# RWKV's inverse placed elsewhere in the program, SiLU and one gate written with tanh, and the first products of a hybrid layer regrouped

## The chip, the cores and the metric

The kernel runs on one core of a Trainium2 chip. The core has five engines with queues of their own: TensorE for matrix products (PE in the profile; PEld are its weight loads), VectorE (DVE), ScalarE (ACT), GpSimd (POOL) and SyncE (SP), which here issues nearly all transfers. Every engine takes its instructions in the order of its queue. The metric is the device time of one execution in microseconds (us); lower is better.

## The reference, cut to what matters

One layer of a decoder with three token mixers on the same input, x of 256 tokens by 2048 channels. One projection of x gives the columns of all mixers and three merge gates:

```python
proj = einsum('bsd,dc->bsc', x, w_in)
z_a, xbc, dt_raw, u_b, z_b, p_rkvz, p_w, p_a, p_gate = split(proj, offs)
# Mamba-2 (SSD): silu(conv(xbc)) gives xs, B, C; y * silu(z_a), then a group norm
# S5: y * sigmoid(y @ w_glu + b_glu) * silu(z_b)
# RWKV-7: r, k, v, z shifted by a token; tanh(xw) @ w2 and xa @ a2 (LoRA); recurrence over tokens; * silu(z)
gates = sigmoid(p_gate + gate_b)
merged = gates[0] * (y_a @ w_a) + gates[1] * (y_b @ w_b) + gates[2] * (y_c @ w_c)
x = layer_norm(alpha * x + merged @ w_out)
```

Here silu(v) = v * sigmoid(v), and sigmoid(v) = (1 + tanh(v / 2)) / 2.

## The kernel before

**Products in three parts.** Every weight column block of 128 is a tile of 2048 x 128 values. `loadw` (line 356) brings it in two halves of 512 KB (`raw`, issued on SP), ScalarE rounds a half to a high part `hi` (line 366), and VectorE subtracts to get the low part `lo` (line 368). x is split the same way once, in eight slabs (`xhi`, `xlo`, lines 308 and 309). `proj` (line 374) then makes 48 products of 128 x 256 into one PSUM tile: hi by xhi, hi by xlo, lo by xhi for 16 slices. There are four buffers each of raw, hi and lo, so two tiles are under way.

**Start.** `setup` (line 298) fetches the slabs of x and, after the first of them, the weights `wd` of the step sizes (32 columns). 48 products of 32 columns give `ps_dt` (lines 317 to 319). The tile `lora`, fetched after x, follows as an ordinary projection (`rwkv_lora`, line 435), then k0, k1 and so on. `par` and `cst`, two tables of constants, are issued at the very start on ScalarE's queue, and five small operations on VectorE prepare scalings from them.

**RWKV.** The 16 heads are worked in four blocks of two pairs. `PROG` (line 81) is the order in which work is emitted: F is a block's front (its projections k, r, v and `rwkv_prep`, which ends in the products `pa` and the masked matrix `Aa`), T the inverse, C the recurrence by chunks, and z, g2 and u are plain projections. In `rwkv_tinv` (line 608) `Aa` goes through DRAM into a layout in which VectorE solves 32 rows one after the other, 31 multiplications `Pm` (line 622) and 31 reductions into `TT` (line 623); the result goes through DRAM again (`Td`, `TTf`); and block products on TensorE, `py` (lines 640 to 649), join the 32 x 32 blocks. Each `py` stands in TensorE's queue at a fixed place, and what stands behind it waits with it. `rwkv_z` (line 711) ends with a SiLU on ScalarE.

**SSD, S5 and the rest.** `PROG2` (line 85) is the order of what follows: S are the eight groups of SSD (`ssd_group`, line 797: four projections x, a convolution, SiLU at line 807, and every other group a block z with SiLU at line 794), s the tiles of S5, zb its gate (SiLU at line 1165), a, b and c the three output branches (`branch`, line 1193; gate a is a sigmoid at line 1202), U the gated unit, G the gates of branch b. ScalarE can evaluate only functions of the table set that it has loaded; `ACT_TABLE_LOAD` changes the set.

**What sets the order.** The program is written for a scheduler that plays it through and places each engine's instructions: what is emitted under `high_priority` (all of `loadw`, shifts, gates) goes first where it is ready, the rest in the order of emission. So an edit in one place can move instructions in others.

Of the kernel before, what the change touches and what calls it, by code (L numbers as in the profile page):

```python
# [1310 lines left out]
```

## Time and profile before

| | us |
|---|---|
| median of 3 runs | 1325.28 (1324.92 to 1326.07) |
| the profiled execution | 1328.45 |
| its span in the trace | 1326.7 |
| PE busy in it | 1278.9 |
| PEld busy | 1202.2 |
| DVE busy | 977.4 |
| ACT busy | 824.0 |

The span runs from the first instruction to the last. A matmul is pipelined: one of 256 columns is shown as 0.28 us long, but the next starts 0.11 us after it, so TensorE can be shown as busy while it waits a little. The granted clock (PEclk) is a share of 2.4 GHz.

### The profile page before, as it was taken

How to read it: one execution, taken by the hardware profiler on the slowest of the kernel's cores; microseconds unless marked ns; L12 is line 12 of the kernel's file. 1: busy time of each engine (PE TensorE's matmuls, PEld its weight loads, DVE VectorE, ACT ScalarE, POOL GpSimd, SP SyncE). 2: the span in 40 equal slices, each digit the busy share in tenths (PEclk: the TensorE clock that was granted, in tenths of full speed). 3: DMA queues.
4: the chain of work that ended last, by engine and by line, in shares of the span. 5: the costliest groups of instructions: out<-in, count | busy, mean ns of one | idle time of the engine just before them, and what ended most of it. 6: DMA issues, size and time to landing. Idle time of an engine off the chain costs nothing.

```text
span 1326.7 us, 27360 instructions
## 1 busy us (share of the span) xinstructions
PE 1278.9 (96%) x10924; PEld 1202.2 (91%) x10924; DVE 977.4 (74%) x1768; ACT 824.0 (62%) x1421; POOL 11.0 (1%) x63
## 2 busy tenths in 40 slices
PE   7999899999999998899999999999999999999996
PEld 7999899999899888798998989999999999999885
DVE  5779887579868646699998656889786665548655
ACT  5677565676645667887768778586655454445430
POOL 1000000000000000000000000000000000000000
PEclk9999999999989998999999999999999999999998
...
GB/s 301 180 167 170 176 161 167 135 133 161 150 170 148 165 150 132 114 191 157 183 171 166 191 165 168 155 152 196 194 176 170 183 184 208 207 225 247 248 176 64
DMA packets 96960, 230.65 MB, mean 174 GB/s; under 512 B 26720, under 2 KB 41536, under 8 KB 96832
## 3 DMA queue, kind: packets, MB, share of 16 engines
...
q10 hardware_dynamic: 432, 0.68, 0.1%
...
HBM read 224.34 MB, written 3.21 MB: 172 GB/s over the span
## 4 chain that ended last, share of the span: by engine, by line
PE 78%; ACT 8%; DVE 5%; DMA 5%; issue 3%; SPq 1%; DVEq 0%; ACTq 0%; POOL 0%; POOLq 0%
PE ps_g L378 7%; PE ps_g L379 7%; PE ps_g L380 7%; PE br L1157 4%; PE br L1156 4%; PE br L1158 4%; PE ps_x L380 2%; PE ps_x L378 2%; PE ps_x L379 2%; PE po L1258 2%; PE po L1259 2%; PE po L1260 2%; PE zq L789 2%; PE zq L790 2%; PE zq L788 2%
## 5 line engine op out<-in xcount | busy, mean ns | idle before, releaser
L378 PE MATMUL ps_g<-xhi,hi_g 128*128 128x256 f32 x768 | 216.2, 281 | 0.0
L379 PE MATMUL ps_g<-xlo,hi_g 128*128 128x256 f32 x768 | 215.2, 280 | 0.0
L380 PE MATMUL ps_g<-xhi,lo_g 128*128 128x256 f32 x768 | 214.7, 280 | 0.0
L368 DVE TENSOR_TENSOR lo_g<-raw_g,hi_g 128x1024 fp32r<-128x1024 f32 x96 | 117.2, 1221 | 63.7 <-ACT hi_g L366 59.4
L366 ACT ACTIVATE hi_g<-raw_g 128x1024 fp32r<-128x1024 f32 x96 | 101.5, 1058 | 93.0 <-PE ps_g L379 70.1
L379 PEld LDWEIGHTS ps_g<-xlo,hi_g 128*128 128x128 f32 x768 | 145.6, 190 | 1.2 <-issue 0.4
L378 PE MATMUL ps_x<-xhi,hi_x 128*128 128x256 f32 x512 | 146.6, 286 | 0.0
L378 PEld LDWEIGHTS ps_g<-xhi,hi_g 128*128 128x128 f32 x768 | 145.4, 189 | 1.3 <-issue 0.4
L380 PE MATMUL ps_x<-xhi,lo_x 128*128 128x256 f32 x512 | 146.3, 286 | 0.0
L380 PEld LDWEIGHTS ps_g<-xhi,lo_g 128*128 128x128 f32 x768 | 145.2, 189 | 0.9 <-issue 0.4
L379 PE MATMUL ps_x<-xlo,hi_x 128*128 128x256 f32 x512 | 144.6, 282 | 0.0
L368 DVE TENSOR_TENSOR lo_x<-raw_x,hi_x 128x1024 fp32r<-128x1024 f32 x64 | 78.2, 1221 | 50.4 <-ACT hi_x L366 50.1
L366 ACT ACTIVATE hi_b<-raw_b 128x1024 fp32r<-128x1024 f32 x64 | 67.6, 1057 | 58.5 <-PE br L1157 33.1
L378 PEld LDWEIGHTS ps_x<-xhi,hi_x 128*128 128x128 f32 x512 | 97.8, 191 | 1.1 <-issue 0.2
L380 PEld LDWEIGHTS ps_x<-xhi,lo_x 128*128 128x128 f32 x512 | 97.5, 190 | 1.0 <-issue 0.2
L379 PEld LDWEIGHTS ps_x<-xlo,hi_x 128*128 128x128 f32 x512 | 97.4, 190 | 0.5
L368 DVE TENSOR_TENSOR lo_b<-raw_b,hi_b 128x1024 fp32r<-128x1024 f32 x64 | 78.2, 1221 | 24.8 <-ACT hi_b L366 23.0
L366 ACT ACTIVATE hi_x<-raw_x 128x1024 fp32r<-128x1024 f32 x64 | 67.5, 1055 | 37.0 <-PE ps_x L379 16.0
L1157 PE MATMUL br<-yh0l,hi_b 128*128 128x256 f32 x256 | 72.2, 282 | 0.0
L1158 PE MATMUL br<-yh0h,lo_b 128*128 128x256 f32 x256 | 72.0, 281 | 0.0
L1156 PE MATMUL br<-yh0h,hi_b 128*128 128x256 f32 x256 | 71.9, 281 | 0.0
L366 ACT ACTIVATE hi_wo<-raw_wo 128x1024 fp32r<-128x1024 f32 x32 | 33.1, 1057 | 42.1 <-PE po L1260 27.3
...
## 6 DMA issues: line engine op xcount, KB each, us to landing
...
```

What stands on the lines that cost most here:

```text
L366: nc.scalar.activation(hi, raw, AF.Copy)
L368: nc.vector.tensor_tensor(lo, raw, hi.bitcast(F32), ALU.subtract)
L378: nc.tensor.matmul(ps, lhsT=hi.k(k), rhs=g.xhi[:, k, :], start=(k == 0), stop=False)
L379: nc.tensor.matmul(ps, lhsT=hi.k(k), rhs=g.xlo[:, k, :], start=False, stop=False)
L380: nc.tensor.matmul(ps, lhsT=lo.k(k), rhs=g.xhi[:, k, :], start=False, stop=(k == NK - 1))
L788: nc.tensor.matmul(ps[tk], lhsT=g.xhi[:, kk, t], rhs=hi.k512(k), start=f0, stop=False)
L789: nc.tensor.matmul(ps[tk], lhsT=g.xhi[:, kk, t], rhs=lo.k512(k), start=False, stop=False)
L790: nc.tensor.matmul(ps[tk], lhsT=g.xlo[:, kk, t], rhs=hi.k512(k), start=False, stop=l0)
L1156: nc.tensor.matmul(ps, lhsT=hi.k(k0 + k), rhs=h, start=(k == 0), stop=False)
L1157: nc.tensor.matmul(ps, lhsT=hi.k(k0 + k), rhs=l, start=False, stop=False)
L1158: nc.tensor.matmul(ps, lhsT=lo.k(k0 + k), rhs=h, start=False, stop=(k == n - 1))
L1258: nc.tensor.matmul(po, lhsT=m[0][:, t], rhs=hi.k512(k), start=f0, stop=False)
```

## The change

1. *Start.* Four products of a zero tile stand first on TensorE. The step sizes' weights are packed into one stationary tile `whl` (32 high columns, 32 low, 64 zero), so that two products a slice take the place of three, and the lora tile is fetched on ScalarE's queue and multiplied in the same loop, slice by slice, as x comes in. `par` and `cst` move behind the slabs and the first weights on SP; the small scalings from them move from VectorE to POOL. The sum of the two step-size halves is made later (`ssd_dt`).
2. *Block products.* `rwkv_tinv` ends with the transfer of `TTf`; `py` is emitted by new entries Y in `PROG`, for blocks 0 and 2 no earlier than a named product of a projection (`BEHIND`) and, with the C after it, at high priority. Front 2 is split into A2 and B2 around them.
3. *SiLU by tanh.* SiLU of the convolution (32 tiles), z of RWKV (8), z of SSD (8) and zb (8) becomes a tanh on ScalarE and one operation more on VectorE, (t + 1) * v, with v halved beforehand; constants make up for factors of two.
4. *Gate a* is a tanh, with the factor taken in later operations.

```diff
-PROG = ("F0 F1 T0 z2 z3 z0 z6 g2_3 z1 C0 T1 g2_1 F2 C1 g2_0 g2_2 g2_4 z4 g2_5 u6 z7 F3 u3 g2_13 g2_14 g2_7 T2 "
-        "g2_15 z5 g2_6 C2 g2_9 g2_8 T3 u5 C3 g2_11 g2_10 u1 u2 u0 u4 u7 g2_12").split()
+PROG = ("F0 F1 T0 z2 z3 z0 z6 g2_3 z1 T1 g2_1 A2 Y0 C0 Y1 B2 C1 g2_0 g2_2 g2_4 z4 g2_5 u6 z7 F3 u3 g2_13 g2_14 g2_7 T2 "
+        "g2_15 z5 g2_6 g2_9 g2_8 u5 g2_11 Y2 C2 T3 Y3 C3 g2_10 u1 u2 u0 u4 u7 g2_12").split()
+BEHIND = {0: ("v4", 23), 2: ("g2_11", 47)}
 PROG2 = ("dt ch S0 S1 S2 S3 c0 c1 s0 c2 s1 c3 c4 c5 c6 c7 c8 c9 c10 c11 c12 s2 c13 c14 c15 S4 S5 S6 zb4 S7 zb0 "
...
+                b = int(st[1:])
+                with tc.high_priority() if b in BEHIND else ExitStack():
+                    with tc.issue_after(g.mms[BEHIND[b][0]][BEHIND[b][1]].ins) if b in BEHIND else ExitStack():
+                        py = rwkv_ty1(g, bts[b], b)
+                    rwkv_ty2(g, bts[b], b, py)
             elif st[0] == "C":
-                rwkv_chunks(g, bts[int(st[1:])], int(st[1:]))
+                with tc.high_priority() if int(st[1:]) in BEHIND else ExitStack():
+                    rwkv_chunks(g, bts[int(st[1:])], int(st[1:]))
             elif st[0] == "g":
                 gate_c(g, int(st.split("_")[1]))
             elif st[0] == "z":
...
-        ps = g.pp.tile([32, T], F32, name="ps_dt", tag="pj", bufs=3)
-        for k in range(NK):
-            nc.tensor.matmul(ps, lhsT=wd[1][:, k, :], rhs=g.xhi[:, k, :], start=(k == 0), stop=False)
-            nc.tensor.matmul(ps, lhsT=wd[1][:, k, :], rhs=g.xlo[:, k, :], start=False, stop=False)
-            nc.tensor.matmul(ps, lhsT=wd[2][:, k, :], rhs=g.xhi[:, k, :], start=False, stop=(k == NK - 1))
...
-    nc.scalar.dma_start(g.par, I["par"])
-    g.cst = g.fix.tile([128, NCST], F32, name="cst")
-    nc.scalar.dma_start(g.cst, I["cst"])
...
+    with tc.high_priority(), tc.tile_pool(name="xp", bufs=1) as xp:
+        zero = xp.tile([128, T], F32, name="zero")
+        nc.vector.memset(zero, 0.0)
+        pz = g.pp.tile([128, T], F32, name="warm", tag="s", bufs=2)
+        nc.scalar.activation(zero[:, 0:1], zero[:, 1:2], AF.Copy)
+        for _ in range(4):
+            nc.tensor.matmul(pz, lhsT=zero[:, 0:128], rhs=zero, start=True, stop=True)
+        wd = xp.tile([128, 16, 32], F32, name="wd")
+        whl = xp.tile([128, 16, 128], F32R, name="whl")
+        nc.gpsimd.memset(whl[:, :, 64:128].bitcast(F32), 0.0)
+        g.adma = nc.scalar.dma_start(wd, I["wdt"])
+        for b in range(8):
...
+            if b == 0:
+                nc.scalar.activation(whl[:, :, 0:32], wd, AF.Copy)
+                nc.vector.tensor_tensor(whl[:, :, 32:64], wd, whl[:, :, 0:32].bitcast(F32), ALU.subtract)
+            if b == 1:
+                g.wlora = loadw(I["wt"][TIDX["lora"]], "lora", eng=nc.scalar)
+        ps = g.pp.tile([128, T], F32, name="ps_dt", tag="pj", bufs=3)
+        pl = g.plora = g.pp.tile([128, T], F32, name="ps_lora", tag="pj", bufs=3)
+        hi, lo = g.wlora
+        for k in range(NK):
+            nc.tensor.matmul(ps, lhsT=whl[:, k, :], rhs=g.xhi[:, k, :], start=(k == 0), stop=False)
+            nc.tensor.matmul(ps, lhsT=whl[:, k, :], rhs=g.xlo[:, k, :], start=False, stop=(k == NK - 1))
+            nc.tensor.matmul(pl, lhsT=hi.k(k), rhs=g.xhi[:, k, :], start=(k == 0), stop=False)
+            nc.tensor.matmul(pl, lhsT=hi.k(k), rhs=g.xlo[:, k, :], start=False, stop=False)
+            nc.tensor.matmul(pl, lhsT=lo.k(k), rhs=g.xhi[:, k, :], start=False, stop=(k == NK - 1))
+        dtx = xp.tile([64, T], F32, name="dtr")
...
+    with tc.issue_after(g.wdma.ins):
+        nc.sync.dma_start(g.par, I["par"])
+        nc.sync.dma_start(g.cst, I["cst"])
...
+    g.hgb = g.fix.tile([128, 88], F32, name="hgb")[:, 0:32]
+    nc.gpsimd.tensor_scalar(g.hgb[:, 0:16], p("gb", 32, 16), 0.5, None, ALU.mult)
+    nc.gpsimd.tensor_scalar(g.hgb[:, 16:32], p("gb", 0, 16), 0.5, None, ALU.mult)
...
+        m = g.mms[n] = []
...
+            m.append(nc.tensor.matmul(ps, lhsT=hi.k(k), rhs=g.xhi[:, k, :], start=(k == 0), stop=False))
...
+def rwkv_ty1(g, bt, b):
+    nc, idn, pys = g.nc, g.c("ident"), []
     for i in range(2):
         py = g.pr.tile([128, 3, NCH, 32], F32, name=f"py{b}_{i}", tag="r", bufs=2)
+        for c in range(NCH):
+            for h, (lo, hi) in enumerate(HS):
+                nc.tensor.matmul(py[lo, 0, c, :], lhsT=bt.TTf[lo, h, i, c, 0:32], rhs=idn[lo, lo], start=True, stop=True)
+        pys.append(py)
+    return pys
...
-    nc.scalar.activation(Z, Z, AF.Silu)
+    t = g.rp.tile([128, T], F32, name=f"zt{hp}", tag="sq2", bufs=2)
+    nc.scalar.activation(t, Z, AF.Tanh)
+    nc.vector.scalar_tensor_tensor(Z, t, 1.0, Z, ALU.add, ALU.mult)
...
-            nc.scalar.activation(g.zs[:, tk, :], ps[tk], AF.Silu)
+            nc.scalar.activation(g.zs[:, tk, :], ps[tk], AF.Tanh, scale=0.5)
+            nc.vector.scalar_tensor_tensor(g.zs[:, tk, :], g.zs[:, tk, :], 1.0, ps[tk], ALU.add, ALU.mult)
 def ssd_group(g, gr):
...
-        nc.scalar.activation(a, a, AF.Silu)
+        th = g.kp.tile([128, T], F32, name=f"th{n}_{gr}", tag="th", bufs=2)
+        nc.scalar.activation(th, a, AF.Tanh)
+        nc.vector.scalar_tensor_tensor(a, th, 1.0, a, ALU.add, ALU.mult)
         cv.append(a)
     if gr % 2 == 0:
...
-            nc.scalar.activation(sg, pg, AF.Sigmoid, bias=g.p("gb", j))
+            nc.scalar.activation(sg, pg, AF.Tanh, scale=0.5, bias=g.hgb[:, 16 + j:17 + j])
     elif br == 1:
         sg = g.sgb[j]
     if j % per == 0:
...
+        elif br == 0:
+            nc.vector.scalar_tensor_tensor(sg, sg, 1.0, pb, ALU.add, ALU.mult)
+            nc.vector.tensor_tensor(acc, acc, sg, ALU.add)
         else:
             nc.vector.tensor_tensor(sg, pb, sg, ALU.mult)
-            if br == 0:
-                nc.vector.scalar_tensor_tensor(acc, acc, 0.5, sg, ALU.mult, ALU.add)
-            else:
-                nc.vector.tensor_tensor(acc, acc, sg, ALU.add)
+            nc.vector.scalar_tensor_tensor(acc, acc, 0.5, sg, ALU.mult, ALU.add)
```

The scheduled orders differ in many places; three matter to the prediction.

VectorE at the end of the first inverse (TT0, Pm0; lo_r4, lo_v4 are low parts of projections, K4 a shift). Before:

```order
L368 TENSOR_TENSOR lo_r4_0_2504<-raw_r4_0_2500,hi_r4_0_2502 128x1024
L622 TENSOR_TENSOR Pm0_1490<-TT0_1489,AT0_1488 128x8x31
L623 TENSOR_REDUCE TT0_1489<-Pm0_1490 128x8
L622 TENSOR_TENSOR Pm0_1490<-TT0_1489,AT0_1488 128x256
L623 TENSOR_REDUCE TT0_1489<-Pm0_1490 128x8
L368 TENSOR_TENSOR lo_r4_1_2510<-raw_r4_1_2506,hi_r4_1_2508 128x1024
L432 SCALAR_TENSOR_TENSOR K4_2410<-ps_k4_2361,par_166,K4_2410 128x255
L368 TENSOR_TENSOR lo_v4_0_2568<-raw_v4_0_2564,hi_v4_0_2566 128x1024
```

After:

```order
L346 TENSOR_TENSOR lo_r4_0_2241<-raw_r4_0_2237,hi_r4_0_2239 128x1024
L677 TENSOR_REDUCE TT0_1484<-Pm0_1485 128x8
L676 TENSOR_TENSOR Pm0_1485<-TT0_1484,AT0_1483 128x8x30
L677 TENSOR_REDUCE TT0_1484<-Pm0_1485 128x8
L676 TENSOR_TENSOR Pm0_1485<-TT0_1484,AT0_1483 128x8x31
L346 TENSOR_TENSOR lo_r4_1_2247<-raw_r4_1_2243,hi_r4_1_2245 128x1024
L474 SCALAR_TENSOR_TENSOR K4_2156<-ps_k4_2107,par_219,K4_2156 128x255
L677 TENSOR_REDUCE TT0_1484<-Pm0_1485 128x8
L676 TENSOR_TENSOR Pm0_1485<-TT0_1484,AT0_1483 128x256
L346 TENSOR_TENSOR lo_v4_0_2305<-raw_v4_0_2301,hi_v4_0_2303 128x1024
L677 TENSOR_REDUCE TT0_1484<-Pm0_1485 128x8
```

The low parts of r4's second half and v4's first, and K4, now stand ahead of the last reductions; farther up, five products `yc <- zt` (the new SiLU) stand between the same two ends as well, so that 123 rows lie there where there were 115.

TensorE at the block products of the same inverse (py0; ps_r4, ps_v4 are projections, ssps5 a norm). Before:

```order
L379 MATMUL ps_r4_2512<-xlo_70,hi_r4_1_2508 128x256
L380 MATMUL ps_r4_2512<-xhi_69,lo_r4_1_2510 128x256
L640 MATMUL py0_0_1567<-cst_168,TTf0_445 32x32
L640 MATMUL py0_1_1599<-cst_168,TTf0_445 32x32
L640 MATMUL py0_0_1567<-cst_168,TTf0_445 32x32 x7
L640 MATMUL py0_1_1599<-cst_168,TTf0_445 32x32 x7
L455 MATMUL ssps5_2486<-ksq5_2484,cst_168 128x256
L378 MATMUL ps_r4_2512<-xhi_69,hi_r4_1_2508 128x256
```

After:

```order
L418 MATMUL ps_v4_2313<-xlo_70,hi_v4_0_2303 128x256
L419 MATMUL ps_v4_2313<-xhi_69,lo_v4_0_2305 128x256
L698 MATMUL py0_0_2365<-cst_220,TTf0_568 32x32 x8
L698 MATMUL py0_1_2374<-cst_220,TTf0_568 32x32 x8
L417 MATMUL ps_v4_2313<-xhi_69,hi_v4_1_2309 128x256
L418 MATMUL ps_v4_2313<-xlo_70,hi_v4_1_2309 128x256
L419 MATMUL ps_v4_2313<-xhi_69,lo_v4_1_2311 128x256
```

They have moved from behind product 42 of r4 to behind product 24 of v4, 30 products of a projection later. From the last `pa` of the pair before to py0 there are 593 of them, where there were 563; for the third inverse (py2) there are 543, where there were 558.

ScalarE in the second group of SSD (csb1 are decays, rs0 a norm, B_1 a SiLU, X3_2 a chunk of RWKV's last block). Before:

```order
L859 ACT_TABLE_LOAD
L859 ACTIVATE csb1_1_6766<-csb1_1_6766 128x512
L872 ACTIVATE sq0_6481,ss0_6480<-y_0_6442 128x256
L694 ACTIVATE Sz1_225<-SVA3_3656 64x2x64 x2
L366 ACTIVATE hi_x5_0_6906<-raw_x5_0_6904 128x1024
L874 ACT_TABLE_LOAD
L874 ACTIVATE rs0_6484<-ss0_6480,ssdeps_5794 128x2
L807 ACT_TABLE_LOAD
L807 ACTIVATE B_1_6691<-B_1_6691 128x256
L666 ACTIVATE X3_2_5206<-ch3_2_5201 128x128
```

After, the same work of that group:

```order
L950 ACTIVATE sq0_6507,ss0_6506<-y_0_6468 128x256
L937 ACTIVATE csb1_1_6800<-csb1_1_6800 128x512
L884 ACTIVATE thC_1_6795<-C_1_6790 128x256
L761 ACTIVATE Sz1_281<-SVA3_3793 64x2x64
L950 ACTIVATE sq0_6507,ss0_6506<-y_0_6468 128x256
L761 ACTIVATE Sz1_281<-SVA3_3793 64x2x64
L952 ACT_TABLE_LOAD
L952 ACTIVATE rs0_6510<-ss0_6506,ssdeps_5805 128x2
L344 ACTIVATE hi_x18_1_7017<-raw_x18_1_7015 128x1024
L880 ACTIVATE xs0_2_6932<-ps_x4_6883,par_219 128x256
L955 ACTIVATE y_0_6468<-y_0_6468,rs0_6510 128x256 x2
L733 ACTIVATE X3_2_5279<-ch3_2_5274 128x128
```

Of three table loads ahead of the chunk's copy X3_2 one is left, and B's SiLU has become a tanh that stands farther up. In the whole program 84 table loads become 41.

## Rows read from the trace of the kernel before

**Rows 1.** The page: engines with busy time, share, instructions; then the chain by engine.

```profile
PE 1278.9 (96%) x10924; PEld 1202.2 (91%) x10924; DVE 977.4 (74%) x1768; ACT 824.0 (62%) x1421; POOL 11.0 (1%) x63
...
PE 78%; ACT 8%; DVE 5%; DMA 5%; issue 3%; SPq 1%; DVEq 0%; ACTq 0%; POOL 0%; POOLq 0%
```

**Rows 2.** Stretches: bounds, length, busy time of PE, PEld, DVE, ACT, POOL, clock, DMA.

```profile
480.00:580.00 100.00, 89.09 (x679) 80.43 (x678) 66.44 (x162) 82.09 (x152) 0.10 (x1) 0.95 0.46 138
580.00:720.00 140.00, 136.26 (x1153) 126.58 (x1152) 134.76 (x293) 100.72 (x207) 1.05 (x10) 1.00 0.57 172
720.00:900.00 180.00, 174.09 (x1429) 164.72 (x1428) 132.55 (x226) 133.16 (x241) 0.53 (x5) 1.00 0.56 165
1060.00:1220.00 160.00, 160.00 (x1380) 160.00 (x1380) 95.04 (x123) 76.78 (x102) 0.00 (x0) 1.00 0.69 216
```

**Rows 3.** Timelines of PE and DVE, 5 to 21 us: start, length, instruction, idle before it.

```profile
5.24 0.69 DVE L309 TENSOR_TENSOR xlo<-xr,xhi 128x512 fp32r<-128x512 f32 x1
...
6.81 0.42 PE L317 MATMUL ps_dt<-xhi,wd 128*32 128x256 f32 x1 [6.81 <-ACT wd L312]
...
11.24 0.28 PE L317 MATMUL ps_dt<-xhi,wd 128*32 128x256 f32 x1
...
20.25 0.28 PE L378 MATMUL ps_k<-xhi,hi_k 128*128 128x256 f32 x1
```

**Rows 4.** First inverse: one stretch of the engines, then PE's timeline.

```profile
98.90:153.50 54.60, 54.13 (x502) 52.12 (x501) 53.29 (x118) 36.91 (x65) 0.21 (x2) 1.00 0.57 170
...
159.88 0.28 PE L380 MATMUL ps_r<-xhi,lo_r 128*128 128x256 f32 x1
...
163.80 0.28 PE L640 MATMUL py<-cst,TTf 32*32 32x32 f32 x4 [3.65 <-DMA TTf<-Td]
```

**Rows 5.** Third inverse: one stretch of the engines, then PE's timeline.

```profile
294.90:354.50 59.60, 59.60 (x572) 57.41 (x567) 57.54 (x121) 41.41 (x70) 1.71 (x6) 1.00 0.53 161
...
364.86 0.22 PE L640 MATMUL py<-cst,TTf 32*32 32x32 f32 x2 [3.20 <-DMA TTf<-Td]
...
366.14 0.48 PE L640 MATMUL py<-cst,TTf 32*32 32x32 f32 x10 [1.06 <-DMA TTf<-Td]
```

**Rows 6.** Stretches in which the granted clock is half; columns as in rows 2.

```profile
164.40:167.80 3.40, 3.40 (x38) 3.16 (x39) 0.00 (x0) 0.72 (x3) 0.00 (x0) 0.50 0.88 197
365.80:372.60 6.80, 6.46 (x60) 6.11 (x60) 0.94 (x1) 3.42 (x9) 0.00 (x0) 0.50 0.59 181
512.60:519.40 6.80, 6.14 (x34) 5.70 (x36) 3.81 (x5) 4.58 (x11) 0.00 (x0) 0.50 0.44 145
563.80:567.10 3.30, 3.30 (x9) 2.63 (x8) 2.75 (x5) 3.27 (x8) 0.00 (x0) 0.50 0.71 182
```

**Rows 7.** Wait of PE: what waited, for whom, total us, times, longest us.

```profile
PE ch L668 <- ACT X L666: 3.7, 1, 3.7
```

**Rows 8.** Groups of DVE by line: count, busy us, mean ns, idle before.

```profile
L309 DVE TENSOR_TENSOR xlo<-xr,xhi 128x512 fp32r<-128x512 f32 x8 | 5.4, 692 | 0.3 <-ACT xhi L308 0.3
...
L368 DVE TENSOR_TENSOR lo_v<-raw_v,hi_v 128x1024 fp32r<-128x1024 f32 x16 | 19.4, 1217 | 6.4 <-ACT hi_v L366 6.2
...
L461 DVE RECIPROCAL ksq<-ksq 128x256 f32<-128x256 f32 x8 | 13.7, 1736 | 2.5 <-ACT ksq L458 2.5
...
L432 DVE SCALAR_TENSOR_TENSOR yc<-ps_z,par,yc 128x255 f32<-128x255 f32 x8 | 3.8, 478 | 0.1
...
L868 DVE TENSOR_TENSOR y<-y,zs 128x512 f32<-128x512 f32 x8 | 5.5, 685 | 0.1
```

**Rows 9.** Groups of ACT by line: count, busy us, mean ns, idle before.

```profile
L807 ACT ACT_TABLE_LOAD x17 | 21.8, 1283 | 2.9 <-DVE xs L806 2.6
...
L859 ACT ACT_TABLE_LOAD x8 | 10.3, 1283 | 0.1
```

**Rows 10.** Convolution, line 806, on DVE: stretch, length, busy (operations), clock, DMA share.

```profile
480.00:580.00 100.00, 11.46 (x24) 0.95 0.46 138
480.00:900.00 420.00, 39.60 (x84) 0.99 0.54 161
```

More of the change, by code (lines that the diff above doesn't have):

```diff
@@ L62, in tile_order @@
     for s in PROG:
-        if s[0] == "F":
+        if s[0] in "FA":
             o += front_tiles(int(s[1:]))
-        elif s[0] not in "CT":
+        elif s[0] not in "CTYB":
             o.append(s)
@@ L354, in setup, with loadw @@
     g.Half = Half
-    def loadw(src, nm, pool=None, parts=1):
+    def loadw(src, nm, pool=None, parts=1, eng=None):
         with tc.high_priority():
@@ L362, in loadw @@
                 raw = pool.tile([128, n, 128], F32, name=f"raw_{nm}_{q}", tag="raw", bufs=WB[0] if pool is g.wp else 4)
[L363 to L364 removed]
+                with tc.issue_after((g.adma if eng else g.wdma).ins) if parts > 1 or eng else ExitStack():
+                    d = (eng or nc.sync).dma_start(raw, src[:, n * q:n * q + n, :])
+                if eng:
+                    g.adma = d
+                else:
+                    g.wdma = d
                 hi = pool.tile([128, n, 128], F32R, name=f"hi_{nm}_{q}", tag="hi", bufs=WB[1] if pool is g.wp else 4)
@@ new lines, in setup, with c, p @@
+    g.par = g.fix.tile([128, NPC], F32, name="par")
+    g.cst = g.fix.tile([128, NCST], F32, name="cst")
+    with tc.issue_after(g.wdma.ins):
+        nc.sync.dma_start(g.par, I["par"])
+        nc.sync.dma_start(g.cst, I["cst"])
+    def c(n):
+        o, w = CST[n]
+        return g.cst[:, o:o + w]
+    g.c = c
+    def p(n, i=0, w=1):
+        return g.par[:, PC[n] + i:PC[n] + i + w]
+    g.p = p
+    g.hgb = g.fix.tile([128, 88], F32, name="hgb")[:, 0:32]
+    nc.gpsimd.tensor_scalar(g.hgb[:, 0:16], p("gb", 32, 16), 0.5, None, ALU.mult)
@@ L436, in rwkv_lora @@
     nc, rp = g.nc, g.rp
-    ps = g.proj("lora")
+    ps = g.plora
     xl = rp.tile([128, T], F32, name="xl", tag="tA")
@@ L462, in head_rs, with rwkv_rv, rwkv_keys @@
     return sq
-def rwkv_front(g, b):
-    nc, rp, tc = g.nc, g.rp, g.tc
+def rwkv_rv(g, hp):
+    rp = g.rp
+    ps = g.proj(f"r{hp}")
+    R = rp.tile([128, T], F32, name=f"R{hp}", tag="R", bufs=2)
+    rwkv_shift(g, ps, g.p("mu", hp), g.omm[:, hp:hp + 1], R)
+    ps = g.proj(f"v{hp}")
+    V = rp.tile([128, T], F32, name=f"V{hp}", tag="V", bufs=2)
+    rwkv_shift(g, ps, g.p("mu", 16 + hp), g.omm[:, 16 + hp:17 + hp], V)
+    return R, V
+def rwkv_keys(g, b):
+    nc, rp = g.nc, g.rp
     K, k2s = [], []
@@ L477, in rwkv_front @@
     bt = Ctx()
+    bt.keys = K, k2s
+    bt.rv = rwkv_rv(g, 2 * b)
+    return bt
+def rwkv_front(g, bt, b):
+    nc, rp, tc = g.nc, g.rp, g.tc
+    K, k2s = bt.keys
     bt.XS, bt.bkT, bt.MTr, bt.bon = [], [], [], []
@@ L646, in rwkv_tinv @@
             nc.scalar.activation(Y[hi, 1], py[hi, 1], AF.Copy)
-        for h, (lo, hi) in enumerate(hs):
+        for h, (lo, hi) in enumerate(HS):
             for c in range(NCH):
@@ L727, in ssd_setup @@
     g.ssdeps = kp.tile([128, 1], F32, name="ssdeps")
-    nc.gpsimd.memset(g.ssdeps, 1e-5)
+    nc.gpsimd.memset(g.ssdeps, 4e-5)
+    for n, w in (("cw", 128), ("cb", 32)):
+        nc.vector.tensor_scalar(g.p(n, 0, w), g.p(n, 0, w), 0.5, None, ALU.mult)
     g.dskb = kp.tile([128, 32], F32, name="dskb")
@@ L735, in ssd_dt @@
     x = g.k1("dtx", (32, T))
-    nc.sync.dma_start(x, g.dtd)
+    xl = g.k1("dtxl", (32, T))
+    nc.sync.dma_start(x, g.dtd[0:32])
+    nc.sync.dma_start(xl, g.dtd[32:64])
+    nc.vector.tensor_tensor(x, x, xl, ALU.add)
     nc.vector.tensor_scalar(x, x, g.par[0:32, PC["dtb"]:PC["dtb"] + 1], None, ALU.add)
```

91 lines of the change are left out of this document (36 added, 55 removed).

## The prediction

> **What bounds the kernel now.** I read the page first, then stretches of it, then what TensorE waits for. On the page [rows 1] the reader sees TensorE busy for 1278.9 us of a span of 1326.7 us, and 78% of the chain that ended last on it. So 47.8 us are all its gaps together, and a change that touches no product can win only from these, from stretches at half clock, and from products that it saves. From 1060 us on there is nothing to win: 160 us of 160 are busy, with 1380 products in them [rows 2], so one costs 160 / 1380 = 0.116 us, the pace used below.
>
> The gaps lie in four places. At the start TensorE has its first product at 6.81 us, and the first one of k0 at 20.25 [rows 3]. At the first inverse it stands still for 3.65 us ahead of `py`, whose operand comes back from DRAM [rows 4], at the third for 3.20 and 1.06 us [rows 5], and each is followed by a granted clock of 0.50, for 3.4 and 6.8 us [rows 6]. That is the level of 1.2 GHz, at which half of the time is lost, 1.7 and 3.4 us. From 480 to 900 us, SSD and S5, TensorE lacks 10.9, 3.7 and 5.9 us in the three stretches, 20.6 us [rows 2]; the largest single wait there is 3.7 us for the copy X on ScalarE [rows 7]; and two stretches at 0.50, 6.8 and 3.3 us [rows 6], lose half, 5.05 us. Together this is 25.6 us, and 16 of them lie before 580. There ScalarE is busy for 82.1 us of 100, VectorE for 66.4; from 580 to 720 it is the other way about, VectorE at 134.8 of 140 [rows 2]. The rest is the tail, which the change leaves alone.
>
> **Start: -3.0.** 48 products of the step sizes become 32, so 32 + 48 = 80 real products stand ahead of k0, 80 x 0.116 = 9.3 us. At best they run without a gap from where the first one starts now: 6.81 + 9.3 = 16.1, 4.1 us sooner than 20.25. At worst lora's second low part decides. VectorE needs eight slabs of x, the packing (a 128 x 512 like them) and two low parts, 9 x 0.692 + 2 x 1.217 = 8.7 us [rows 8]; counted from 5.24, where its first slab is [rows 3], that ends at 13.9. Then slices 8 to 15 follow, 40 products or 4.6 us, to 18.5, 1.7 us sooner. Between the two I take the middle, 17.3, since neither end is nearer to a row: -3.0. The zero products add four products ahead of the first real one, in time that is idle; if they don't raise the clock, the early products cost 0.42 us on the trace instead of 0.28 as now [rows 3], and that is inside the worse end. The small scalings on POOL are hidden, for POOL is busy for 11 us in all [rows 1]. `par` and `cst` come later; the first product that needs them is the norm of k0, behind k0's own 48 products, 5.6 us, so I price that at nothing; what it came later than these 5.6 us would be paid in full.
>
> **First inverse: +1.8.** VectorE is the bound between the first `Pm` and the last reduction: busy 53.29 us of 54.60 [rows 4]. Whatever is put in there delays the transfers of `TT` and so `py`. The order puts in five `yc` operations and K4, 6 x 0.478 = 2.87 us, and the low parts of r4's second half and of v4's first, 2 x 1.217 = 2.43 us [rows 8]: 5.3 us in all. The other side of it is that TensorE meets `py0` 30 products later, 3.5 us. The wait of 3.65 us grows by 5.3 - 3.5 = 1.8 us. What is queued behind it is v4, and so the whole program. The bounds: everything gone, -3.65 - 1.7 of half clock = -5.4; and +3.5, if the longer wait brings the loss of the half clock, 1.7, a second time.
>
> **Third inverse: +4.9.** VectorE again: 57.54 of 59.60 us busy [rows 5]. By the orders there come in one reciprocal (1.74), three `yc` (1.43) and one low part (1.22), and there go out a scan, taken at a 128 x 512 (0.69), and a shift (0.48) [rows 8]: +3.2 us. Here TensorE has 15 products fewer on its way, 1.7 us sooner at `py2`. Together 4.9 us. The bounds: gone, -4.26 - 3.4 = -7.7; and +8.3, with the loss of 3.4 a second time. The named product behind which `py2` may not start isn't what it waits for: by the order it stands 33 products farther on, in g2_10. For block 0 it stands exactly there.
>
> **SSD and S5: -17.** 84 table loads become 41. A load takes 1.283 us, and ahead of eight of them ScalarE was idle for 0.1 us in all [rows 9], so ScalarE gets back 43 x 1.283 = 55 us, most of it between 430 and 930. A tanh takes the place of a SiLU one for one. On VectorE come, from 480 to 900 us, one operation for each tile of the convolution, 84 / 3 = 28 [rows 10], 6 of z and 7 of zb; with the durations of rows of the same shapes [rows 8] these are 28 x 0.478 + 6 x 0.685 + 7 x 0.478 = 20.8 us, of which 8 x 0.478 + 2 x 0.685 = 5.2 before 580 (24 / 3 = 8 tiles there), where VectorE has 33 us to spare, and 5.2 from 580 to 720, where it has 5.2 [rows 2]. Before 580 ScalarE is the busier engine and its copy X has the largest wait, behind three table loads of which one is left; so I give three quarters of the 16 us there, 12. After it I give half of 9.65 us, since VectorE's queue is full up to 720: 4.8. The bounds are half of the first alone, -8, and all of the 25.6.
>
> Of table loads the Trainium skill says more: "ScalarE: Activation LUTs", section "What ACT_TABLE_LOAD costs", gives a switch of tables a drain of about 1.38 us beside the 1.283 us. The trace agrees on the load and shows no such gap ahead of it [rows 9]. By the page, as an estimate, ScalarE would get back 43 x 2.66 = 114 us, the whole 25.6 us would be nearer than 17, and the forecast 1303.
>
> **Gate a and the other gates: 0.** The added operations on VectorE lie from 930 us on, where TensorE is full and VectorE is busy for 95 us of 160 [rows 2]; without that cover, 16 x 0.48 = 8 us.
>
> **Sum.** -3.0 + 1.8 + 4.9 - 17 = -13.3. On the profiled execution, 1328.45 us with a span of 1326.7, that is 1315; the median of the runs shown is 1325.28, 3.2 us less, and I forecast a median: 1325.3 - 13.3 = **1312**.
>
> **Rival 1: the block products are hidden.** The wait at both inverses goes, as it would if later products cover the transfers, or if the delay on VectorE is smaller than I count (its 1.3 and 2 us of idle [rows 4, 5] take up little of it). Then 3.65 + 1.7 + 4.26 + 3.4 = 13.0 us go instead of 6.7 coming: 1325.3 - 3.0 - 13.0 - 17 = 1292, and with the whole 25.6 1284. For it: the first one is moved by 3.5 us against a wait of 3.65. Against it: VectorE's full rows, and that the third isn't moved back at all.
>
> **Rival 2: VectorE pays, slower.** From 580 to 900 it takes 15.6 us more (5.2 and 10.4), and only the 5.2 us of idle up to 720 take any of it; 10.4 us are then added, because its queue is the one that TensorE waits for, while ScalarE's savings bring only 5 us before 580: 1325.3 - 3.0 + 6.7 + 10.4 - 5 = 1334. It decides as soon as less than about 4 of the 17 us arrive. For it: 134.8 of 140 us [rows 2]. Against it: from 720 on VectorE has 47 us to spare, and the wait that was largest was for ScalarE [rows 7].
> "TensorE: Matmul & The Clock Gate", in its Specs, row "Engine queue depth", states (the Trainium skill) that VectorE and ScalarE take their queues strictly in order, which is what this rival needs; the order of the queue here can be read, and what waits in it from 580 on the trace shows only as a busy share.
>
> **How the numbers follow.** The forecast, 0.58: its ends are the better bounds of start and SSD with the inverses as summed, 1325.3 - 4.1 + 6.7 - 25.6 = 1302, and the worse ones throughout, 1325.3 - 1.7 + 3.5 + 8.3 - 8 = 1327. Rival 1, 0.26. Rival 2, 0.11. What is left, 0.05, is that terms cancel to within 0.2% of 1325.3, 2.7 us, about what a measurement of this kernel can tell from no change. Faster is 0.58 + 0.26 = 0.84, same 0.05, slower 0.11. The range goes from 1289, which leaves out the quarter of rival 1 that lies below, 0.07, to 1324, which leaves out rival 2, 0.11, and little of the forecast, 0.02.
>
> **What would show it.** First product of k0 near 17.3 us instead of 20.25. A wait ahead of `py0` of about 5.5 us and ahead of `py2` of about 9 in all, each with its stretch at half clock; if these are gone, rival 1 holds. From 480 to 580 TensorE busy for about 97 us with 41 table loads in the program; from 580 to 720 a VectorE of 140 us. The forecast is wrong if TensorE stands still for longer in 580 to 900 than the 9.65 us of now, or if a wait comes in the part from 20 to 480 us where none of these terms lies.

## The result, and the profile after

The changed kernel takes 1305.47 us (median of 4 runs, 1302.54 to 1307.12) against 1325.4 of the kernel before beside it: a ratio of 0.9846, 95% interval 0.9831 to 0.9861, 19.9 us less. On another chip it took 1305.71 against 1328.22 (0.9833, 0.9808 to 0.9858). The forecast of 1312 had the right sign and 13.3 of the 19.9 us; the time lies inside its range. The profiled execution is the fastest of the four, 1302.54 us with a span of 1300.6; against the profiled one of before, 1328.45, that is 25.9 us, which is more than the medians differ.

The page of the changed kernel, its engines, as the first line of [rows 1]:

```profile
PE 1268.7 (98%) x10916; PEld 1195.2 (92%) x10916; DVE 995.7 (77%) x1823; ACT 768.5 (59%) x1379; POOL 14.8 (1%) x72
```

TensorE has 10.2 us less of busy time and the span is 26.1 us shorter, so its gaps went from 47.8 to 31.9 us. The stretches that answer to [rows 2], columns as there:

```profile
480.00:580.00 100.00, 96.16 (x786) 88.88 (x787) 82.32 (x196) 79.28 (x165) 0.10 (x1) 1.00 0.54 165
580.00:720.00 140.00, 135.86 (x1165) 126.37 (x1164) 134.64 (x288) 90.70 (x190) 1.05 (x10) 1.00 0.57 172
720.00:900.00 180.00, 176.84 (x1496) 167.89 (x1495) 153.39 (x291) 122.33 (x249) 0.84 (x8) 1.00 0.57 173
```

From 480 to 580 us TensorE is idle for 3.8 us (10.9 before), from 580 to 720 for 4.1 (3.7), from 720 to 900 for 3.2 (5.9). No stretch at half clock is left between the start and the tail; before there were four [rows 6]. At the inverses, TensorE's timeline, first (against [rows 4]) and third (against [rows 5]):

```profile
163.16 0.22 PE L698 MATMUL py<-cst,TTf 32*32 32x32 f32 x2 [1.72 <-DMA TTf<-Td]
163.60 0.69 PE L698 MATMUL py<-cst,TTf 32*32 32x32 f32 x30 [0.23 <-DMA TTf<-Td]
```

```profile
364.53 0.28 PE L698 MATMUL py<-cst,TTf 32*32 32x32 f32 x4 [0.91 <-DMA TTf<-Td]
...
368.35 0.69 PE L698 MATMUL py<-cst,TTf 32*32 32x32 f32 x28 [1.21 <-DMA TTf<-Td]
```

`py0` waits 1.72 us where it waited 3.65, and a second time for 0.23 us (0.24 before), so 1.95 in all where there were 3.89; `py2` waits 2.12 us where it waited 4.26. The start, TensorE's timeline, against [rows 3]:

```profile
3.21 3.78 PE L360 MATMUL warm<-zero 128*128 128x256 f32 x8 [3.21 <-ACT zero L358]
...
7.58 0.55 PE L382 MATMUL ps_dt<-xhi,whl 128*128 128x256 f32 x1 [0.60 <-DVE whl L374]
...
12.18 0.28 PE L386 MATMUL ps_lora<-xhi,lo_lora 128*128 128x256 f32 x1
...
18.87 0.28 PE L417 MATMUL ps_k<-xhi,hi_k 128*128 128x256 f32 x1
```

The products of the zero tile end at 6.99 us, the first one of x comes at 7.58, and one costs 0.28 us on the trace, the sign of the full clock, only from 12.18 on (0.41 us until then; PEclk reads 1.00 in this stretch all the same, so the length of the products is the only sign). A product of k0 stands at 18.87, but the scheduler mixes the first ones with lora's last; a cleaner mark is the first `pa`, at 59.57 us where it was 61.88.

| where the time of the two profiled executions differs | us |
|---|---|
| start, up to the first `pa` | -2.3 |
| first inverse: waits, half clock | -1.9, -1.7 |
| third inverse: waits, half clock | -2.1, -3.4 |
| 480 to 900 us: TensorE idle, half clock | -9.4, -5.05 |
| a new wait of a chunk at 296.91 us | +1.8 |
| sum, of 26.1 | -24.1 |

The last 2.0 us are spread over small gaps that I have not followed.

### The profile page after: what moved, and what is told of

Same layout as the page of the kernel before. It is cut to its first block, busy times and chain, and to the rows that moved or that the text cites. A ratio compares the mean times of both kernels' runs of the same rounds, so it can differ in the third digit from the quotient of the medians.

```text
span 1300.6 us, 27378 instructions
## 1 busy us (share of the span) xinstructions
PE 1268.7 (98%) x10916; PEld 1195.2 (92%) x10916; DVE 995.7 (77%) x1823; ACT 768.5 (59%) x1379; POOL 14.8 (1%) x72
## 3 DMA queue, kind: packets, MB, share of 16 engines
q10 hardware_dynamic: 576, 1.36, 0.3%
## 4 chain that ended last, share of the span: by engine, by line
PE 80%; DVE 7%; ACT 6%; DMA 3%; issue 2%; SPq 1%; DVEq 0%; POOL 0%; ACTq 0%; POOLq 0%
PE ps_g L418 6%; PE ps_g L417 6%; PE ps_g L419 6%; PE br L1235 4%; PE br L1234 4%; PE br L1236 4%; PE ps_x L417 3%; PE ps_x L418 3%; PE ps_x L419 3%; PE po L1337 2%; PE po L1338 2%; PE po L1339 2%; PE zq L865 2%; PE zq L864 2%; PE zq L863 2%
## 5 line engine op out<-in xcount | busy, mean ns | idle before, releaser
L419 PE MATMUL ps_x<-xhi,lo_x 128*128 128x256 f32 x512 | 143.6, 280 | 0.0
L346 DVE TENSOR_TENSOR lo_b<-raw_b,hi_b 128x1024 fp32r<-128x1024 f32 x64 | 78.8, 1231 | 21.6 <-ACT hi_b L344 19.6
L676 DVE TENSOR_TENSOR Pm<-TT,AT 128x16 f32<-128x16 f32 (+30 forms) x124 | 50.8, 410 | 11.6 <-POOL AT L672 5.8
```

Of the source, the lines that this page charges most:

```text
L346: nc.vector.tensor_tensor(lo, raw, hi.bitcast(F32), ALU.subtract)
L419: m.append(nc.tensor.matmul(ps, lhsT=lo.k(k), rhs=g.xhi[:, k, :], start=False, stop=(k == NK - 1)))
L676: nc.vector.tensor_tensor(Pm[:, :, 0:n], TT[:, :, 0:n], col, ALU.mult)
```

## The experiments

Ratios are to the kernel before on the same chip, with 95% intervals; on these three chips its medians were 1327.14, 1327.37 and 1328.22 us.

**The changed kernel once more (e11).** Beside the ratio given above, its profile shows the same waits: `py0` 1.30 and 0.80 us, `py2` 1.18 and 1.18, the chunk 1.80.

> The changed kernel itself, unaltered, beside the kernel before and the next run on the same chip. If the differences of the other runs against the kernel before hold, its ratio is 0.983 to 0.987 (1305 to 1310 us); it also shows which of its waits come back in every execution: py0 1.5 to 2.1 us, py2 about 1 and 1.2, the chunk's chy about 2 at 297 us, ST about 2.9 at 566 us, and k0 and the first pa at 18 to 19.7 and 58.4 to 60.4 us.

So these are properties of the program; what changes from one execution to the next is the clock, which here was at half for three stretches of 3.4 us in the span (none in the profile above).

**SiLU and sigmoid back on ScalarE (e1).**

```diff
-        nc.scalar.activation(th, a, AF.Tanh)
-        nc.vector.scalar_tensor_tensor(a, th, 1.0, a, ALU.add, ALU.mult)
+        nc.scalar.activation(a, a, AF.Silu, scale=2.0)
...
-            nc.scalar.activation(sg, pg, AF.Tanh, scale=0.5, bias=g.hgb[:, 16 + j:17 + j])
+            nc.scalar.activation(sg, pg, AF.Sigmoid, bias=g.p("gb", j))
```

(and the same for z, zs and zb)

> The changed kernel with SiLU and the sigmoid of gate a as functions of ScalarE again (convolution, z of RWKV and of SSD, zb, gate a), the rest of the change kept. Theory (the table loads carry the larger part): TensorE's idle time in 480 to 900 us goes from 11.1 back to about 20 us, with stretches at half clock there again, +14 us in all; the eight products of yc leave the inverses, up to -2 us: 1317 to 1320 against 1305.5 of the changed kernel. Rival (the gain lies in the places of the block products and the start): 1308 or less.

1329.36 us, ratio 1.0014 (0.9998 to 1.003): the whole gain is gone, about 9 us more than I expected. Its stretches:

```profile
480.00:580.00 100.00, 91.33 (x716) 83.07 (x713) 70.02 (x162) 86.42 (x162) 0.26 (x2) 0.97 0.50 149
580.00:720.00 140.00, 135.14 (x1135) 125.92 (x1133) 133.76 (x301) 98.53 (x204) 1.16 (x11) 0.98 0.57 168
720.00:900.00 180.00, 173.02 (x1401) 163.92 (x1400) 130.00 (x216) 132.54 (x236) 0.43 (x4) 0.98 0.54 161
```

TensorE is idle for 20.5 us in 480 to 900, as before the change, and the granted clock falls to half there for three stretches of 6.8 us (two of 6.8 and 3.3 before), so 20.5 + 10.2 = 30.7 us are lost against 25.6. Against the changed kernel that is 19.6 us of the 25.8 by which the span is longer. The longest single wait there is again the one for the copy X, as in [rows 7]:

```profile
PE ch L735 <- ACT X L733: 3.8, 1, 3.8
```

Most of the rest is at the first inverse, VectorE, ScalarE and TensorE in one list (2.4 us more are waits at the fourth one):

```profile
165.94 0.18 DVE L676 TENSOR_TENSOR Pm<-TT,AT 128x16 f32<-128x16 f32 x1 [6.37 <-DMA raw_g<-in_wt]
...
166.49 0.42 ACT L500 ACTIVATE ksq<-ksq 128x256 f32<-128x256 f32 x1 [7.39 <-DVE ksq L499]
...
167.76 0.25 ACT L709 ACTIVATE Yl<-py 32x128 f32<-32x128 f32 x1
...
168.34 0.63 PE L712 MATMUL py<-Yl,Aoff 32*32 32x32 f32 x8 [3.27 <-ACT Yl L709]
```

Here VectorE comes to the second inverse early and stands for 6.37 us at its first `Pm`, because the operands aren't there. Behind it in its queue is the norm `ksq`; for that ScalarE stands 7.39 us, and behind it in ScalarE's queue is `Yl`, the copy between two steps of the block products; for that TensorE stands 3.27 us, and 6.8 us at half clock follow. Without the tanh the moved block products win nothing at the first inverse: the wait has gone one step farther. At the third there is 0.99 us of wait and 3.4 us at half clock, where there were 4.26 and 6.8. The Trainium skill ("TensorE: Matmul & The Clock Gate", Specs, row "Engine queue depth") says that VectorE and ScalarE take their queues strictly in order; these rows agree.

**The tanh forms alone (e2)**, on the old start, with the block products emitted straight behind the inverse.

```diff
-PROG = ("F0 F1 T0 z2 z3 z0 z6 g2_3 z1 T1 g2_1 A2 Y0 C0 Y1 B2 C1 ...
-BEHIND = {0: ("v4", 23), 2: ("g2_11", 47)}
+PROG = ("F0 F1 T0 Y0 z2 z3 z0 z6 g2_3 z1 C0 T1 Y1 g2_1 F2 C1 ...
+BEHIND = {}
```

> The other way round: only the tanh forms, with the old start and with the block products emitted straight behind the inverse as in the kernel before (the scheduler then places py0 599 products behind the last pa, py2 561; 576 and 572 in the kernel before, where py0 and py2 are counted with all products of 256 columns). Theory: 1325.4 - 14 and something for the inverses, 1308 to 1312. Rival: over 1318.

1314.82, ratio 0.9894 (0.9875 to 0.9914): by the ratios -14.0 us alone, but -22 on top of the other parts (e1 against the changed kernel). TensorE's idle time in 480 to 900 is 11.8 us, with no half clock; with 25.6 us lost there before, the 14 are won in SSD and S5.

**SiLU for the convolution alone (e12)**, the first of the two edits of e1.

> The changed kernel with SiLU for the convolution alone (32 tiles); z of RWKV and of SSD, zb and gate a stay with tanh. 62 table loads in the program (41 in the changed kernel, 85 with all of SiLU and the sigmoid back). Theory (it is the number of loads in 430 to 830 us, where the convolution stands, that costs): 21 of the 44 loads come back, so about half of the 22 us that the whole undoing cost, 9 to 13 us above the changed kernel, most of it in 480 to 580 us. Rival (one function of another set left in the path costs as much as all): 18 us or more. Rival (the gain is VectorE's or RWKV's, not the convolution's loads): under 4.

1319.37, ratio 0.9945 (0.9928 to 0.9962), 13.7 us above the changed kernel beside it. Its stretches:

```profile
480.00:580.00 100.00, 92.70 (x721) 84.50 (x720) 69.95 (x152) 83.85 (x162) 0.26 (x2) 0.97 0.51 152
580.00:720.00 140.00, 135.11 (x1124) 126.78 (x1122) 130.33 (x287) 97.01 (x192) 0.94 (x9) 0.99 0.58 170
720.00:900.00 180.00, 174.04 (x1487) 164.46 (x1486) 146.84 (x285) 130.95 (x260) 0.84 (x8) 1.00 0.56 166
```

TensorE's idle time is 7.3 + 4.9 + 6.0 = 18.2 us, against 3.9 + 2.2 + 3.9 = 10.0 in the changed kernel beside it (e11). Of this difference 3.4 us lie before 580, where ScalarE's busy time rises from 77.4 to 83.9 us, and a stretch of 6.8 us at half clock, 3.4 us more, is added there. 21 of 44 table loads carry 13.7 of 22 us. That is more than the 9 to 13 expected, but the two ratios leave about 4 us either way, so the runs don't tell it from half. In this run the added waits end with VectorE (10.1 of the 18.2 us, 2.8 of 10.0 in e11), the largest being

```profile
PE br L1232 <- DVE xs L882: 2.9, 1, 2.9
```

VectorE itself waits for ScalarE's high parts hi_x for 25.7 us in 480 to 900, against 16.6 in e11 and 37.2 in the kernel before. So the loads can reach TensorE by way of VectorE; but each of these edits also lets the scheduler place other instructions anew, and no run separates the two.

**The block products by emission (e3)**, the same PROG as above, on the new start.

> The changed kernel, with the block products emitted straight behind the inverse and the chunks in their old order (no named product, no high priority). py0 then stands 599 products behind the last pa, 607 in the changed kernel. Theory (the wait is the difference of VectorE's queue plus the way through DRAM, and TensorE's distance): 8 products are 0.9 us, so the waits at py0 and py2 together are 4 to 6 us against 4.1, and the time is 1305 to 1309. Rival (the named place and the high priority of the chunks bring the gain at the inverses): over 1310.

1309.99, ratio 0.9863 (0.984 to 0.9885). `py0` waits 3.22 us, `py2` 3.14 and 1.36, 7.7 us together and more than the 4 to 6 expected. Between this and the changed kernel (0.9846) the intervals overlap; the differences in the two pairs (e2 to e4, e3 to the changed kernel) are 2.2 and 1.7 thousandths, the same way both times, 2 to 3 us, which neither pair alone tells from nothing.

**The old start (e4)** in the changed kernel.

> The changed kernel with the start of the kernel before (48 products of 32 columns, lora as an ordinary projection behind x, par and cst first on ScalarE's queue, no zero products). Theory: k0 starts at 20.25 us instead of 18.87, so +1.4: 1306 to 1308. Rival (the term as predicted): +3, 1308.5. If the zero products and the regrouping do nothing beyond run-to-run differences: 1305.5.

1311.98, ratio 0.9872 (0.985 to 0.9894), 2.6 thousandths or 3.4 us above the changed kernel; e2 against e3 is 3.1 thousandths: more than the 1.4 us expected, and near the term as predicted. The first `pa` stands at 61.88, 62.04, 62.45 and 62.30 us in the four kernels with the old start (mean 62.17), and at 59.57, 60.20, 58.80, 60.43, 58.41, 59.30 and 57.99 in the seven profiles with the new one (mean 59.24): -2.9 us.

**Without the zero products (e5).**

```diff
-        for _ in range(4):
-            nc.tensor.matmul(pz, lhsT=zero[:, 0:128], rhs=zero, start=True, stop=True)
```

> The changed kernel without the four products of the zero tile at the start (and without the memset and the copy that feed them). Theory: they bring nothing, because the first product of x comes at 7.6 us all the same and the granted clock rose at about 12 us with them, at 10.8 in the kernel before without them: k0 starts within 0.5 us of 18.9 and the time is that of the changed kernel, 19 to 21 us below the kernel before. Rival (they bring the clock up earlier): k0 starts 1 to 2 us later, and so does everything else.

1310.4, ratio 0.9865 (0.9847 to 0.9883). First `pa` at 60.05, 0.8 us above the mean of the seven. I was wrong on the clock: the first product of 0.28 us stands at 13.23 us here, and at 7.6 to 9.3 in six of the seven profiles with the zero products (two fell back to half, PEclk 0.50, for 3.4 us after it); the profile of the changed kernel, with 12.18, is the exception. Whether the 2 to 4 us in the ratio are theirs stays open: the intervals touch, and the start shows less.

**The way through DRAM (e6)**, in the kernel before: the transfers `Td` first.

```diff
-    for cs in range(4):
-        r = slice(32 * cs, 32 * cs + 32)
-        nc.sync.dma_start(bt.Td[:, cs], TT[r])
+    with g.tc.high_priority():
+        for cs in range(4):
+            r = slice(32 * cs, 32 * cs + 32)
+            nc.sync.dma_start(bt.Td[:, cs], TT[r])
```

> The kernel before, with the four transfers of TT to DRAM (Td) given high priority, so that SP issues them one behind the other in the first inverse, ahead of the weights raw_r and of two transfers AT, and not two and two around them; little else moves (py0 is split, its first four products ten places earlier). Theory (what stands in SP's queue between the last reduction and the return sets the length of the way through DRAM): from the last reduction to the issue of TTf it goes from 8.1 to 5.6 to 6.2 us, and py0 comes 2 us sooner after the last reduction than 10.35. Rival (the way is fixed, or shorter in the changed kernel for another cause): it stays within 0.5 us of 8.1 and 10.35. In the time, no more than 0 to 4 us less than the kernel before.

First the kernel before: VectorE's last reduction, then SP's queue (SPq: time of issue, length, transfer, count):

```profile
153.03 0.42 DVE L623 TENSOR_REDUCE TT<-Pm 128x8 f32<-128x256 f32 x1
...
153.91 0.88 SPq L626 DMA_DIRECT2D Td<-TT  x2
...
154.83 0.42 SPq L364 DMA_DIRECT2D raw_r<-in_wt  x1
...
155.30 0.90 SPq L626 DMA_DIRECT2D Td<-TT  x2
...
156.25 0.89 SPq L616 DMA_DIRECT2D AT<-Ad  x2
...
157.23 0.37 SPq L364 DMA_DIRECT2D raw_v<-in_wt  x1
...
161.55 1.80 SPq L631 DMA_DIRECT2D TTf<-Td  x4
```

and the changed kernel:

```profile
154.54 0.43 DVE L677 TENSOR_REDUCE TT<-Pm 128x8 f32<-128x256 f32 x1
...
155.34 1.83 SPq L680 DMA_DIRECT2D Td<-TT  x4
...
157.27 0.37 SPq L338 DMA_DIRECT2D raw_v<-in_wt  x1
...
158.05 0.30 SPq L670 DMA_DIRECT2D AT<-Ad  x1
...
160.56 1.80 SPq L685 DMA_DIRECT2D TTf<-Td  x4
```

Before, a weight stands among the four `Td`, two transfers `AT` and a weight behind them, and from the end of the last reduction (153.45) to the issue of `TTf` it is 8.1 us; after the change the four `Td` stand together, and it is 5.6 (from 154.97). The experiment, the last reduction, SP, and TensorE:

```profile
154.75 0.42 DVE L623 TENSOR_REDUCE TT<-Pm 128x8 f32<-128x256 f32 x1
...
155.64 1.80 SPq L627 DMA_DIRECT2D Td<-TT  x4
...
159.39 0.32 SPq L632 DMA_DIRECT2D TTf<-Td  x1
...
159.80 0.40 SPq L364 DMA_DIRECT2D raw_v<-in_wt  x1
...
160.24 1.42 SPq L632 DMA_DIRECT2D TTf<-Td  x3
...
163.49 0.28 PE L641 MATMUL py<-cst,TTf 32*32 32x32 f32 x4 [2.18 <-DMA TTf<-Td]
...
167.35 0.87 PE L641 MATMUL py<-cst,TTf 32*32 32x32 f32 x24 [1.20 <-DMA TTf<-Td]
```

The first `TTf` is issued 4.2 us after the reduction, the others 5.1, and `py0` starts 8.3 us after it, not 10.35: for the way out, up to the issue of `TTf`, the order on SP is the cause. The other profiles agree: in e1, where a weight again stands among the four `Td`, it is 8.3 us; in the nine in which the four stand together, the changed kernel's two among them, 5.6 to 6.3. For the whole way it is not shown: a weight now stands between the `TTf`, and the last of `py0` starts 12.2 us after the reduction, 10.9 before. In the time it brings nothing (1328.06, ratio 0.9997, 0.9981 to 1.0013): `py0` waits 2.18 + 1.20 us, and 6.8 us at half clock follow, where there were 3.4.

**Block products later (e7).**

```diff
-BEHIND = {0: ("v4", 23), 2: ("g2_11", 47)}
+BEHIND = {0: ("v4", 41), 2: ("g2_10", 47)}
```

> The changed kernel with the block products 18 products later in the first inverse (behind product 42 of v4) and, in the third, all behind the end of g2_10 (13 to 28 products later; g2_10 is emitted ahead of them). Theory (TensorE's distance counts one for one, 0.116 us a product): the wait of 2.0 us at py0 goes to 0 to 0.3, the 2.1 us at py2 to under 1, and nothing behind waits for it: 2 to 4 us below the changed kernel. Rival (the chunks, moved with them, come too late and the wait turns up at their own products or in SSD): the same time as the changed kernel or more.

1311.58, ratio 0.9879 (0.9864 to 0.9894), slower than the changed kernel. At the first inverse, TensorE, ScalarE, TensorE:

```profile
162.78 0.21 PE L698 MATMUL py<-cst,TTf 32*32 32x32 f32 x2 [0.54 <-DMA TTf<-Td]
...
174.31 0.42 ACT L587 ACTIVATE EE<-L 128x256 f32<-128x256 f32 x1 [3.68 <-DVE L L583]
...
175.69 0.27 ACT L713 ACTIVATE Yl<-py 32x128 f32<-32x128 f32 x1
...
176.01 0.43 PE L716 MATMUL py<-TTf,Yl 32*32 32x32 f32 x8 [2.06 <-ACT Yl L713]
```

The wait for `TTf` fell from 1.95 to 0.87 us, and 2.06 us turned up at the third step: `Yl` stands behind `EE` in ScalarE's queue, which waits 3.68 us for VectorE's L. At the third inverse one wait of 2.49 us took the place of two. More than in these waits the time went at half clock, four stretches near 298, 370, 578 and 861 us that cost 10.2 us, against 5.1 in e11. The scheduler also put in 46 table loads instead of 41, so the run is not a test of the place alone. The place in the changed kernel is better than this later one; that it is better than the earlier one (e3) is not told from nothing.

**The convolution's added operation on GpSimd (e9).**

```diff
-        nc.vector.scalar_tensor_tensor(a, th, 1.0, a, ALU.add, ALU.mult)
+        nc.gpsimd.tensor_scalar(th, th, 1.0, None, ALU.add)
+        nc.gpsimd.tensor_tensor(a, th, a, ALU.mult)
```

> The changed kernel with the added operation of the convolution, (t + 1) * v, made by GpSimd in two operations, so that VectorE has 32 operations of 128 x 256 less in 430 to 830 us. If VectorE's queue is what kept 580 to 720 us from gaining (idle of TensorE 3.74 before, 4.14 after), VectorE is busy for under 132 us of 140 there and TensorE idle for about 3, so 1 to 3 us are gained. If the waits there are for something else, or if GpSimd takes longer for the two than VectorE for the one by more than its cover, the time stays or grows by up to 10 us.

1315.86, ratio 0.9912 (0.9895 to 0.9928), 9 to 10 us slower than the changed kernel. GpSimd's groups (count, busy us, mean ns, idle before) and the stretch from 580 us:

```profile
L885 POOL TENSOR_SCALAR thxs<-thxs 128x256 f32<-128x256 f32 x16 | 21.9, 1369 | 184.9 <-ACT thxs L884 176.7 <-DVE lo_x L346 8.2
...
L886 POOL TENSOR_TENSOR xs<-thxs,xs 128x256 f32<-128x256 f32 x16 | 18.8, 1177 | 1.3
...
580.00:720.00 140.00, 134.81 (x1134) 125.29 (x1136) 133.19 (x278) 87.48 (x184) 20.16 (x23) 0.99 0.57 168
```

Two operations take 1.37 + 1.18 us in the mean for x (1.11 to 1.19 and 0.98 to 1.17 for B and C) where VectorE's one took 0.43, in front of everything that needs B, C and x. VectorE is still busy for 133.2 of 140 us and TensorE idle for 5.2: relief of VectorE by 8 operations did not shorten this stretch. What holds it stays open.

## Why the forecast was right, and where its steps were not

- *Start, -3.0.* Right in size: -2.9 by the mean of the profiles. The mark that I named, k0 at 17.3 us, was not; it stands at 18.87 (17.3 to 19.7 in the seven profiles with the new start), and is mixed with lora's products.
- *First inverse, +1.8; measured -1.9, and -1.7 of half clock.* The step that failed is "the wait of 3.65 us grows by 5.3 - 3.5". VectorE's share was near: the inverse takes 58.45 us instead of 54.57, 3.9 of the 5.3 counted. Its idle time there stayed (1.3 and 1.2 us); the eight operations cost less than the sum of their durations, because one of them starts about 0.1 us before the one ahead of it ends, and (t + 1) * v takes 0.41 us there, not 0.478. TensorE's 3.5 us held: from the first `Pm` to its arrival at `py0` it is 64.92 us instead of 61.27, 3.65 more. The third length, from the last reduction through DRAM to `py0`, I took as fixed: it went from 10.35 to 8.19 us, because in the new order no weight stands among the `Td` any more. The wait of 3.65 becomes 3.65 + 3.88 - 3.65 - 2.16 = 1.72; the trace has 1.72.
- *Third inverse, +4.9; measured -2.1, and -3.4 of half clock.* VectorE 63.56 instead of 59.60 us, 4.0 for 3.2 counted. The ways through DRAM failed here too, both of them: from the last reduction to `py2` 8.4 instead of 10.4 us, and in, from the last `pa` to the first `Pm`, 8.85 instead of 12.7. SP, POOL and VectorE before, and then SP and VectorE after, with the wait of the chunk below:

```profile
287.19 1.25 SPq L616 DMA_DIRECT2D AT<-Ad  x3
...
288.54 0.37 SPq L364 DMA_DIRECT2D raw_g<-in_wt  x1
...
288.95 0.43 SPq L616 DMA_DIRECT2D AT<-Ad  x1
...
290.52 3.37 DVE L461 RECIPROCAL ksq<-ksq 128x256 f32<-128x256 f32 x2 [1.32 <-ACT ksq L458]
...
294.65 0.16 POOL L618 MEMSET AT<- 128x32 f32 x1 [24.77 <-DMA AT<-Ad]
...
294.88 0.16 DVE L622 TENSOR_TENSOR Pm<-TT,AT 128x16 f32<-128x16 f32 x1
```

```profile
287.90 1.71 SPq L670 DMA_DIRECT2D AT<-Ad  x4
...
292.56 0.18 DVE L676 TENSOR_TENSOR Pm<-TT,AT 128x16 f32<-128x16 f32 x1 [0.39 <-POOL AT L672]
...
294.59 1.74 DVE L503 RECIPROCAL ksq<-ksq 128x256 f32<-128x256 f32 x1
...
296.91 0.27 PE L744 MATMUL chy<-MTr,SVA 128*64 128x64 f32 x1 [1.81 <-ACT SVA L737]
```

Before, a weight stands ahead of the fourth `AT`; after, the four are issued together, and POOL's row, which waits for them, comes at 292.36 instead of 294.65. But VectorE too was busy up to 294.88 before, with two reciprocals ahead of the first `Pm`; after, one of the two stands behind it. It is the reciprocal that the prediction counted as coming into the inverse, without counting that the inverse can then begin sooner. So the inverse began 2.3 us earlier, by the order on SP and by VectorE's together; no run separates the two. On the way out the order was the same in both kernels, three `Td`, a weight, the fourth (354.60 to 356.84 before, 356.24 to 359.11 after), and from the last reduction to the first `TTf` it took 8.6 us before and 6.6 after, 6.9 in e6 and 5.7 in e1 in the same order: why it was shorter stays open. TensorE, with 1.8 us of wait for a chunk's SVA at 296.91, came later. From the first `Pm` to TensorE's arrival at `py2` it is 4.3 us more than before, not 1.7 less: 3.2 + 4.0 - 2.0 - 4.3 = 0.9 for the first of the two waits, 0.91 on the trace.
- *SSD and S5, -17; measured -14.5.* By stretch: 12 forecast before 580 and 7.1 + 5.05 = 12.1 measured; 4.8 forecast after it and 2.4 measured, nothing of it before 720. The reason holds as far as tested: e1 and e2 tie the gain to the tanh forms, and e12, with about half of the loads back, has half of the loss or somewhat more; that it is the loads and not the order placed anew is argued, not separated. The waits of TensorE that end with ScalarE fell from 16.3 to 7.4 us in 480 to 900, and the one for X is gone. ScalarE got 55 us back, of which 14 (alone) to 22 (on top of the rest) shortened the program. The 114 us estimated from the Trainium skill's figure ("ScalarE: Activation LUTs", "What ACT_TABLE_LOAD costs") show nowhere: ScalarE's busy time fell by 55.5 us, no gap stands ahead of a load [rows 9], and the time fell by less than by the loads alone.
- *Gate a, 0.* The count was wrong: VectorE has two operations there before and after, so there was nothing to hide. No run takes this part alone.
- *Rival 1* (1292) was half right: in both profiles of the changed kernel the half clock at the inverses went, and half of each wait. *Rival 2* did not happen: 580 to 720 neither won nor lost (4.1 against 3.7 us), with VectorE at 134.6 of 140 as before [rows 2], and 720 to 900 won although VectorE rose by 21 us.
- *A wait where no term lies.* The chunk's 1.8 us is the sign against itself that the prediction named, a wait between 20 and 480 us outside its terms. It stands in all ten profiles of the changed kernel and its variants, 1.7 to 1.8 us near 296 to 301, with SiLU back (e1), with the block products by emission (e2, e3) and with the old start (e2, e4) too, so it needs none of these parts, and its cause is open.
- The forecast came out 6.5 us too high because the two inverses were 15.8 us off one way in this profile (6.7 forecast, -9.1 measured), and the smaller gain in SSD, the new wait of the chunk and clock losses in the timed runs, which this profile does not have, went the other way. That the time lies inside the range is in part luck: two of the four terms of the sum, those of the inverses, had the wrong sign, and the range was 35 us wide. Parts of the change are not additive, -14 for the tanh alone and -22 on top, which no sum of terms from one trace could show.
